# Layer two's memory attention between the first pair's projections, twelve gates last, and eight heads' sample state updated in the output stage

## The chip, the cores and the metric

The kernel runs on one core of one Trainium2 chip. The metric is the device time of one execution in microseconds (us), the median of several runs. A profile is taken of one further execution; its span is the time from that execution's first to its last instruction. Engines are named as in the profile: PE is TensorE, DVE is VectorE, ACT is ScalarE, POOL is GpSimd, SP is SyncE, which issues the loads.

## The reference, cut to what matters

One step of a two-layer trunk over 256 prompt tokens and 8 sample tokens (264 together), width 2048. Layer one mixes tokens by windowed attention; layer two, which the change is about, by a gated recurrence with 12 heads. Each layer has four memory heads beside that, a gate of the full width and an output projection:

```python
q, f, iv, mq, g = split(h @ w_in)                  # 12 + 12 + 12 + 4 + 16 column blocks of 128
fg = lb + (1 - lb) * sigmoid(f);  k = 1 - fg;  q = silu(q)
o, s_new = chunked recurrence over q, k, iv, log(fg), from s0      # prompt: s0 = 0; sample: s0 = state_hgrn
o = o * rsqrt(mean(o * o) + eps) * norm_w
mem_o = softmax(mq @ mk.T / sqrt(128)) @ mv        # prompt: mk, mv projected; sample: from the caches
y = (concat(o, mem_o) * silu(g)) @ w_out
h = layer_norm(ALPHA * h + y)
```

For a sample token the recurrence has one step: `s_new[b] = fg * s0[b] + k * v` for each of 8 sequences and 12 heads (a 128x128 matrix each). These 96 matrices are an output of the step. The token's own result needs `s0`, but not `s_new`.

## The kernel before, in words

**Units.** Almost all work is cut into units of one load each: 1 MB of weights or of a memory cache, or 512 KB of sample state. `Stream` (the class of lines 58 to 131) holds them in a list. A unit's load goes through the SP queue into one of four "raw" buffers in on-chip memory. `prep` then splits the float32 values into a high and a low half-precision part: ACT scales and rounds (line 97), DVE subtracts (line 98). The parts go to one of four "hl" buffers, or, for the last eight output units, to one of eight "held" buffers. PE multiplies with three passes (lines 303 to 305): high by high, high by low, low by high. A weight unit is 16 chunks of three matmuls with 264 columns. A raw buffer is free for another load when its split is done. A state unit's raw buffer is kept longer, as its new state is made in place and stored from there by POOL.

**Order.** The list gives the order in which units are written. A scheduler then places each instruction on its engine by its own simulated time, so neighbouring units mix, and it also picks which of the four raw buffers a load gets. On the chip every engine works through its list in order. The SP queue does too: a load that must wait for its buffer holds up all loads behind it. `pump` starts the next piece of side work (recurrence of a head pair, memory softmax of a head) after each unit.

**Layer two before.** Six pairs of heads come one after the other: f, f, v, v, then per head q, state and (heads 0 to 7) an early gate. `state_unit` computes the sample token's result from the state and then updates the state: 8 matmuls that spread v over partitions (`vb`, line 1233), 8 ACT scalings (line 1237), 8 DVE multiply-adds (line 1238), and the store. After the pairs come the four memory-query units, then eight cache units (`c_mk`, `c_mv`) which alternate with the eight late gates, and the memory softmax. A cache unit is split like a weight unit, but its 32 matmuls have one or two columns. The last stage is 16 output units: the projection (matmuls `o`), a residual addition (line 747) and two running sums (lines 764 and 765) on DVE. Output units 8 to 15 run first over 176 columns and, from the held buffers, again over the remaining 88 while the first part is normalised.

## Time and profile before

| | |
|---|---|
| median of 3 runs | 905.26 us (904.99 to 907.28) |
| the profiled execution's own time | 906.08 us |
| its span, first to last instruction | 904.3 us |
| busy: PE / DVE / ACT / POOL | 886.6 / 701.5 / 582.4 / 34.9 us |
| moved by DMA | 198.67 MB, 220 GB/s on average |

Layer two's first unit starts on PE at 420 us. The matmuls of the cache units (`mss`, `mso`) and of the late gates around them lie between about 729 and 803 us, and those of the output units (`o`) between 800 and 893 us. Matmuls are pipelined, so that a busy PE only says that some matmul was under way. The number of matmuls that started in a stretch says how fast PE really went. Below, rows give busy us in a window with the number of instructions behind it, or, for groups of instructions, the number, the busy time and the mean duration.

### The profile page before, as it was taken

What the parts mean: (1) busy time and instruction counts of PE and PEld (TensorE: products, weight loads), DVE (VectorE), ACT (ScalarE), POOL (GpSimd) and SP (SyncE); (2) the same over time, 40 slices, a digit from 0 to 9 for tenths busy, and PEclk for the clock granted to TensorE, in tenths of its full rate; (3) what the DMA queues carried; (4) which work ended last, traced back from release to release, by engine and by line L of the source; (5) the groups of instructions that cost most, each with busy time, mean ns of one, the idle gap of its engine ahead of it and who ended that gap; (6) DMA issues with size and microseconds to landing.
All of it is one profiled execution on the core that took longest, in us unless ns stands there. A gap on an engine that the chain in (4) does not pass through costs nothing.

```text
span 904.3 us, 21814 instructions
## 1 busy us (share of the span) xinstructions
PE 886.6 (98%) x9281; PEld 762.9 (84%) x9281; DVE 701.5 (78%) x1230; ACT 582.4 (64%) x982; POOL 34.9 (4%) x68
## 2 busy tenths in 40 slices
PE   9999999999999999999999999999999999799996
PEld 6888889678888888876888888898888888688996
DVE  6879877669886666697687887979788989678736
ACT  6767776657664444476766877777777585858415
POOL 1100010000000000002000000000000000000000
PEclk9999999999999999999999999999999999899999
DMA  9998566557785555556374655827454878456303
GB/s 340 392 353 317 188 245 209 188 208 265 262 333 192 187 192 203 207 198 214 127 292 137 216 201 174 299 101 260 160 215 164 303 283 308 172 207 244 130 2 97
DMA packets 37853, 198.67 MB, mean 220 GB/s; under 512 B 4555, under 2 KB 10732, under 8 KB 17532
## 3 DMA queue, kind: packets, MB, share of 16 engines
q1 hardware_dynamic: 33024, 181.55, 56.3%
q0 software_dynamic: 4688, 15.67, 4.6%
q8 instruction: 72, 1.18, 0.5%
q14 instruction: 25, 0.20, 0.1%
q10 hardware_dynamic: 44, 0.07, 0.0%
HBM read 180.03 MB, written 17.22 MB: 218 GB/s over the span
## 4 chain that ended last, share of the span: by engine, by line
PE 77%; DVE 8%; ACT 6%; DMA 6%; issue 3%; SPq 0%; ACTq 0%; DVEq 0%
PE o L303 5%; PE o L305 5%; PE o L304 5%; PE g L305 5%; PE g L303 5%; PE g L304 5%; DVE hl L98 4%; ACT hl L97 2%; PE hv L305 2%; PE hv L303 2%; PE hv L304 2%; DMA raw<-in_w_in 2%; PE hq L303 2%; PE hq L305 2%; PE hq L304 2%
## 5 line engine op out<-in xcount | busy, mean ns | idle before, releaser
L98 DVE SCALAR_TENSOR_TENSOR hl<-raw,hl 128x2048 f16<-128x2048 f32 (+2 forms) x168 | 358.6, 2138 | 82.0 <-ACT hl L97 81.0
L97 ACT ACTIVATE hl<-raw 128x2048 f16<-128x2048 f32 (+2 forms) x168 | 299.2, 1784 | 97.8 <-PE o L305 45.4
L305 PEld LDWEIGHTS <-hl 128*128 128x128 f16 (+2 forms) x2048 | 197.4, 98 | 31.8 <-DVE hl L98 2.9
L303 PEld LDWEIGHTS <-hl 128*128 128x128 f16 (+2 forms) x2048 | 197.3, 98 | 30.6 <-issue 2.2
L304 PEld LDWEIGHTS <-hl 128*128 128x128 f16 (+2 forms) x2048 | 197.4, 98 | 30.3 <-issue 2.2
L305 PE MATMUL g<-xhl,hl 128*128 128x264 f16 x512 | 142.0, 277 | 2.4 <-DVE hl L98 2.4
L303 PE MATMUL g<-xhl,hl 128*128 128x264 f16 x512 | 141.9, 277 | 0.0
L304 PE MATMUL g<-xhl,hl 128*128 128x264 f16 x512 | 141.9, 277 | 0.0
L303 PE MATMUL o<-mix,hl 128*128 128x264 f16 x384 | 105.4, 276 | 0.8 <-DVE xres L747 0.8
L304 PE MATMUL o<-mix,hl 128*128 128x264 f16 x384 | 105.8, 276 | 0.0
L305 PE MATMUL o<-mix,hl 128*128 128x264 f16 x384 | 105.7, 276 | 0.0
L303 PE MATMUL q<-xhl,hl 128*128 128x264 f16 x192 | 53.0, 276 | 1.0 <-DVE kst L251 1.0
L303 PE MATMUL f<-xhl,hl 128*128 128x264 f16 x192 | 52.9, 276 | 0.4 <-DVE mvhl L251 0.4
L305 PE MATMUL hv<-xhl,hl 128*128 128x264 f16 x192 | 53.0, 276 | 0.0
L303 PE MATMUL hq<-xhl,hl 128*128 128x264 f16 x192 | 53.0, 276 | 0.0
L304 PE MATMUL hq<-xhl,hl 128*128 128x264 f16 x192 | 53.0, 276 | 0.0
L305 PE MATMUL hq<-xhl,hl 128*128 128x264 f16 x192 | 53.0, 276 | 0.0
L304 PE MATMUL hv<-xhl,hl 128*128 128x264 f16 x192 | 53.0, 276 | 0.0
L303 PE MATMUL hv<-xhl,hl 128*128 128x264 f16 x192 | 53.0, 276 | 0.0
L304 PE MATMUL q<-xhl,hl 128*128 128x264 f16 x192 | 53.0, 276 | 0.0
L305 PE MATMUL q<-xhl,hl 128*128 128x264 f16 x192 | 53.0, 276 | 0.0
L304 PE MATMUL f<-xhl,hl 128*128 128x264 f16 x192 | 52.9, 276 | 0.0
(338 smaller groups left out, 1858.4 us busy)
## 6 DMA issues: line engine op xcount, KB each, us to landing
raw<-in_w_in SPq DMA_DIRECT2D x88, 1024.0 KB, 6.4
raw<-in_w_o SPq DMA_DIRECT2D x32, 1024.0 KB, 5.0
raw<-in_w_mk SPq DMA_DIRECT2D x8, 1024.0 KB, 4.9
raw<-in_w_mv SPq DMA_DIRECT2D x8, 1024.0 KB, 4.9
raw<-in_c_mk SPq DMA_DIRECT2D x8, 1024.0 KB, 5.1
raw<-in_c_mv SPq DMA_DIRECT2D x8, 1024.0 KB, 7.0
raw<-in_state SPq DMA_DIRECT2D x12, 512.0 KB, 5.4
out_ss<-raw POOLq DMA_DIRECT2D x12, 512.0 KB, 5.5
```

The lines of the kernel that those rows point to most:

```text
L97: hi = self.nc.scalar.activation(hl[:, 0, s], raw[:, s], AF.Copy, scale=scale)
L98: lo = self.nc.vector.scalar_tensor_tensor(hl[:, 1, s], raw[:, s], scale, hl[:, 0, s], op0=ALU.mult, op1=ALU.subtract)
L303: mm(out, lhs(0), rhs(0), start=start, stop=False)
L304: mm(out, lhs(0), rhs(1), start=False, stop=False)
L305: return mm(out, lhs(1), rhs(0), start=False, stop=stop)
```

## The change

It does four things, all in layer two.

1. The four memory-query units stand right behind head 0's f unit. The eight cache units stand among the other projections of heads 0 and 1: ck0, f1, ck1, ck2, v0, ck3, v1, q0, cv0, cv1, gate 0, cv2, cv3, q1, then the two state units. The prompt's memory softmax moves with them.
2. Early gates are left for heads 0, 2, 3 and 6. The other twelve gates come after the last pair, with 10 and 11 at the end.
3. Heads 4 to 11 don't update their sample state in `state_unit`. They store what the update needs (v rows, forget gate, key; 80 floats per partition) to device memory. Eight update units stand in the output stage, one after each of output units 0, 2, ... 14. Each loads the head's state a second time (512 KB) and the stored 40 KB into a raw buffer, and does the same 8 matmuls, 8 scalings, 8 multiply-adds and store as before. State units of these heads no longer hold their raw buffer.
4. When more than one piece of side work is waiting, two steps are pumped after a unit.

```diff
-NG1 = 8
+EARLY = (0, 2, 3, 6)
+LATER = tuple(range(4, HD))
+KEPT = P // 2 + 2 * TS
...
     def load(self, i):
...
+            if s is None:
+                for home, src in self.units[i][0]:
+                    self.nc.sync.dma_start(home(t), src)
+                continue
...
+    def update(h, R, vr, fgs, ks8, sel):
+        for g in range(2):
+            pvb = bank("pt", 2, f"vb{h}{g}")
+            for bb in range(4):
+                mm(pvb[:, bb * P : (bb + 1) * P], sel[:, 4 * g + bb], vr, start=True, stop=True)
+            for bb in range(4):
+                b = 4 * g + bb
+                s = R[:, b]
+                nc.scalar.activation(s, s, AF.Copy, scale=fgs[:, b : b + 1])
+                nc.vector.scalar_tensor_tensor(
+                    s, pvb[:, bb * P : (bb + 1) * P], ks8[:, b : b + 1], s, op0=ALU.mult, op1=ALU.add
+                )
+        nc.gpsimd.dma_start(ss_o[h // 2, :, h % 2 * TS * P : (h % 2 + 1) * TS * P], R.rearrange("p b v -> p (b v)"))
...
+    def update_unit(h):
+        def fn(raw):
+            if not late_sel:
+                late_sel.append(cp.tile([P, TS, P], F16, tag="ms", name="late_sel", bufs=2))
+                nc.sync.dma_start(late_sel[0], sel_d)
+            R = raw[:, : TS * P].rearrange("p (b v) -> p b v", b=TS)
+            k = raw[:, TS * P : TS * P + KEPT]
+            update(h, R, k[:, : P // 2].bitcast(F16), k[:, P // 2 : P // 2 + TS], k[:, P // 2 + TS :], late_sel[0])
...
+            if h in LATER:
+                tail = cur["vr"][:, i, P // 2 :]
+                nc.vector.tensor_copy(tail[:, :TS], fgs)
+                nc.vector.tensor_copy(tail[:, TS:], ks8)
+                nc.gpsimd.dma_start(kept[pi][:, i], cur["vr"][:, i])
+                return
+            update(h, R, vr, fgs, ks8, H["sel"])
...
+    w1("f", 0, f_unit(0))
+    for h in range(NM):
+        w1("mq", h, mem1_sides(mq_unit(h)) if h == NM - 1 else mq_unit(h))
+    cache(c_mk, ck_unit, 0)
+    w1("f", 1, f_unit(1))
+    cache(c_mk, ck_unit, 1)
+    cache(c_mk, ck_unit, 2)
+    w1("v", 0, hv_unit(0))
+    cache(c_mk, ck_unit, 3)
+    w1("v", 1, hv_unit(1))
+    w1("q", 0, hq_unit(0))
+    cache(c_mv, cv_unit, 0)
+    cache(c_mv, cv_unit, 1)
+    gate_of(0)
+    cache(c_mv, cv_unit, 2)
+    cache(c_mv, cv_unit, 3)
+    w1("q", 1, hq_unit(1))
+    state_of(0)
+    state_of(1)
...
     for i in range(NC):
         stream.add(wb(w_o[1], i), out_unit(1, i), home=hold if i >= NC - NSPLIT else None)
+        if i % 2 == 0 and i // 2 < len(LATER):
+            h = LATER[i // 2]
...
+            stream.add(srcs, update_unit(h), split=False)
...
-        pump(1)
+        pump(2 if len(side) > 1 and i > state_at[1] else 1)
```

How the order of instructions moves is shown at three places. In the rows, the number behind a load (`raw170`) is the unit's place in the whole list. In matmul outputs, `o18` is output unit 8 of layer two and `g110` its gate 10; lines of the new program are 8 to 13 higher than those of the old.

The first place is the SP queue in the output stage, with what each load waits for. Before, only weights stand there:

```order
L79 DMA raw166_11485<-in_w_o 128x2048
L79 DMA raw167_11544<-in_w_o 128x2048
L79 DMA raw168_11607<-in_w_o 128x2048
L79 DMA raw169_11666<-in_w_o 128x2048
L79 DMA raw170_11725<-in_w_o 128x2048
L79 DMA raw171_11784<-in_w_o 128x2048
```

Now, from output unit 9 (`raw170`) to output unit 13 (`raw176`):

```order
L88 DMA raw170_11650<-in_w_o 128x2048 [waits DMASW5_49,PE_49]
L88 DMA raw171_11652<-in_w_o 128x2048 [waits DMAHW2_49,DVE_49]
L86 DMA raw172_11654<-in_state 128x1024 [waits DMAHW7_49,DMAHW5_49,DVE_49]
L86 DMA raw172_11654<-kept4_95 128x80 [waits DMAHW0_49,DMASW6_49]
L88 DMA raw173_11798<-in_w_o 128x2048 [waits DMASW6_49,PE_49]
L88 DMA raw174_11800<-in_w_o 128x2048 [waits DMAHW6_49,DVE_49]
L86 DMA raw175_11802<-in_state 128x1024 [waits DMAHW3_49,DMAHW1_49,DVE_49]
L86 DMA raw175_11802<-kept5_96 128x80 [waits DMAHW4_49,DMASW7_49]
L88 DMA raw176_11946<-in_w_o 128x2048 [waits DMASW7_49,PE_49]
```

Between the output weights stand the state and the stored rows of heads 9 and 10. The loads of output units 9, 11 and 13 wait on a DMASW semaphore, which is a store by POOL: their raw buffers are those of the updates of heads 6, 7 and 8.

The second place is ACT around the last gates. The rows run from the Ln of the last pair's normalisation to gate 11; `hl158` and `hl159` are the splits of output units 1 and 2, and `raw160` is the update of head 5:

```order
L1193 ACT_TABLE_LOAD
L1193 ACTIVATE osq50_10801<-rms50_10865,eps_rms_83 128x264
L743 ACT_TABLE_LOAD
L743 ACTIVATE sil115_10990<-g115_10941 128x264
L106 ACTIVATE hl158_11051<-raw158_10808 128x2048
L1193 ACT_TABLE_LOAD
L1193 ACTIVATE osq51_10803<-rms51_10868,eps_rms_83 128x264
L1196 ACT_TABLE_LOAD
L1196 ACTIVATE osq50_10801<-osq50_10801 128x264
L1215 ACTIVATE raw160_10938<-raw160_10938 128x128 x8
L739 ACTIVATE mix_99<-sil115_10990 128x264
L1196 ACTIVATE osq51_10803<-osq51_10803 128x264
```

The normalisation of heads 10 and 11, which stood in the middle of the cache units before, now runs while PE does the last two gates, and two of these rows belong to other work: gate 15's tanh and the scalings of head 5's update.

The third place is DVE at the end of the value-cache units, in the first pair. `hl97` is the split of the last of them, `hl98` that of head 1's q, `hl99` to `hl101` those of the two states and of head 2's f:

```order
L1059 COPY vr0_6264<-hvr0_6362 128x128
L107 SCALAR_TENSOR_TENSOR hl97_6540<-raw97_6288,hl97_6540 128x2048
L744 SCALAR_TENSOR_TENSOR mix_99<-mix_99,g10_6582 128x264
L261 SCALAR_TENSOR_TENSOR mphl13_6427<-mpt13_6422,mphl13_6427 128x512
L1059 COPY vr0_6264<-hvr1_6499 128x128
L107 SCALAR_TENSOR_TENSOR hl98_6577<-raw98_6368,hl98_6577 128x2048
L710 TENSOR_REDUCE msos1_6703<-mso1_6507 128x32
L107 SCALAR_TENSOR_TENSOR hl99_6633<-raw99_6441,hl99_6633 128x1024
L107 SCALAR_TENSOR_TENSOR hl100_6668<-raw100_6505,hl100_6668 128x1024
L107 SCALAR_TENSOR_TENSOR hl101_6706<-raw101_6543,hl101_6706 128x2048
```

Head 1's q is split only behind the copy of its transposed v (`hvr1`), which PE makes near the end of the value-cache matmuls. Before, the last value-cache unit was followed by gates alone, and the states of heads 0 and 1 stood apart.

More of the change, by code (lines that the diff above doesn't have):

```diff
@@ L72, in parts @@
         n = 4 if i == 0 else 2 if i < 4 else 1
-        w = self.units[i][0].shape[1] // n
+        src = self.units[i][0]
+        if isinstance(src, list):
+            return [None]
+        w = src.shape[1] // n
         return [slice(k * w, (k + 1) * w) for k in range(n)]
@@ L1241, in fn, with w1 @@
-            nc.gpsimd.dma_start(ss_o[pi, :, i * TS * P : (i + 1) * TS * P], raw)
+            if h in LATER:
[5 more added lines that the diff above has]
+            update(h, R, vr, fgs, ks8, H["sel"])
         return fn
     state_at = {}
-    for pi in range(HD // 2):
+    def w1(part, i, fn):
+        stream.add(wb(w_in1, NB1[part] + i), fn)
@@ new lines, in state_of, with gate_of, cache, mem1_sides @@
+    def state_of(h):
+        state_at[h] = len(stream.units)
+        stream.add(state[h // 2][:, (h % 2) * TS * P : (h % 2 + 1) * TS * P], state_unit(h), SA, whole=h not in LATER)
+    def gate_of(h):
+        w1("g", h, early_gate(h) if h in EARLY else gate_unit(1, h))
+    def cache(c, unit, t):
+        stream.add(c[1, t], unit(1, t), SA)
+    def mem1_sides(fn):
+        return with_side(fn, [lambda h=h: memp_side(1, h) for h in range(NM)])
+    w1("f", 0, f_unit(0))
+    for h in range(NM):
+        w1("mq", h, mem1_sides(mq_unit(h)) if h == NM - 1 else mq_unit(h))
@@ L1247, in trunk_kernel @@
+    cache(c_mk, ck_unit, 0)
[14 more added lines that the diff above has]
+    state_of(1)
+    for pi in range(1, HD // 2):
         for part, unit in (("f", f_unit), ("v", hv_unit)):
@@ L1248, in trunk_kernel @@
             for i in range(2):
[L1249 removed]
+                w1(part, 2 * pi + i, unit(2 * pi + i))
         for h in (2 * pi, 2 * pi + 1):
[L1251 to L1255 removed]
```

56 lines of the change are left out of this document (19 added, 37 removed).

## The prediction, made before the changed kernel was run

> **What bounds the kernel now.** I read the first part of the page, then the busy times by stage, then PE's waits in the stage that stood out, then the chain of waits there.
>
> ```profile
> span 904.3 us, 21814 instructions
> PE 886.6 (98%) x9281; PEld 762.9 (84%) x9281; DVE 701.5 (78%) x1230; ACT 582.4 (64%) x982; POOL 34.9 (4%) x68
> ```
>
> PE is busy nearly always, so work taken from DVE or ACT is worth only what PE waits for it. The change leaves the matmuls as they are. The stages (columns: busy us of PE, weight loads, DVE, ACT, POOL, with counts; PE's granted clock; DMA share; GB/s) say where PE waits:
>
> ```profile
> 300.00:350.00 50.00, 50.00 (x447) 43.49 (x445) 33.62 (x39) 21.88 (x20) 0.00 (x0) 1.00 0.55 193
> 600.00:650.00 50.00, 50.00 (x534) 44.26 (x532) 42.93 (x85) 37.25 (x68) 1.61 (x3) 1.00 0.58 194
> 700.00:750.00 50.00, 49.96 (x592) 44.45 (x590) 44.63 (x77) 34.38 (x39) 1.61 (x3) 1.00 0.79 289
> 750.00:800.00 50.00, 44.50 (x517) 37.54 (x515) 42.70 (x65) 34.68 (x55) 0.54 (x1) 0.93 0.67 247
> 800.00:850.00 50.00, 49.23 (x451) 43.01 (x450) 40.31 (x45) 32.71 (x33) 0.00 (x0) 1.00 0.56 208
> 850.00:860.00 10.00, 10.00 (x135) 10.00 (x133) 4.78 (x14) 1.47 (x4) 0.00 (x0) 1.00 0.01 2
> ```
>
> The head pairs (600 to 650) leave PE no idle time, with two state updates and two gates per pair. The cache units with late gates (750 to 800) do: PE is idle for 5.5 us and its clock is 0.93, which costs another 0.07 x 50 = 3.5 us. The output stage loses 0.8 us. In it DVE is done early: from 850 us on almost nothing is loaded.
>
> PE's waits from 740 to 805 us, and the chain of waits there (start, us, what):
>
> ```profile
> PE g L305 <- DVE hl L98: 2.4, 2, 1.7
> PE hpo L1169 <- ACT st L1147: 1.5, 1, 1.5
> PE mback L677 <- DVE mrows L674: 1.0, 1, 1.0
> ```
>
> ```profile
> 754.59 4.40 DVE hl L98 x2
> 761.20 2.21 DVE hl L98
> ...
> 776.41 1.28 ACT L1183
> 777.71 0.85 ACT osq L1183 x2
> ```
>
> DVE is the bound, with splits of 2.2 us each. Behind them come the last pair's normalisation and the memory softmax, all late at once. The change spreads exactly this: the cache units go between projections, and the last pair's tail gets twelve gates of PE work for cover.
>
> **The change part by part.** *The cache stage* goes: -5.5 - 3.5 = **-9.0 us**. Twelve gates remain. Per gate PE needs 48 x 50/447 = 5.4 us, DVE one split and three operations of 0.43 like the second row below, 3.5 us, so nothing else waits. The output stage's 0.8 us is counted anew below: **-0.8**.
>
> ```profile
> L733 ACT ACTIVATE sil<-g 128x264 f32<-128x264 f32 x5 | 1.9, 383 | 4.4 <-PE g L305 4.4
> L734 DVE SCALAR_TENSOR_TENSOR sil<-sil,g 128x264 f32<-128x264 f32 x5 | 2.2, 431 | 0.0
> 602.90 0.23 DVE L1049 COPY vr<-hvr 128x128 f16<-128x128 f16 x1 [1.99 <-PE hvr L1048]
> L747 DVE SCALAR_TENSOR_TENSOR xres<-xres,o 128x176 f32<-128x176 f32 (+1 forms) x8 | 2.8, 348 | 14.6 <-PE o L305 14.6
> ```
>
> *The pairs* lose eight updates from DVE and ACT and gain two small copies and a 40 KB store by POOL per head; PE is covered there already (50.00 busy of 50), so 0. Without cover the copies would be some 0.2 us each, by the third row. Pumping two steps also costs 0 here: the pairs without a gate keep 5.4 us units to hide a step.
>
> *The first pair* takes in the eight cache units. A cache unit's 32 matmuls take little of PE. Windows with many of them:
>
> ```profile
> 774.00:778.00 4.00, 2.88 (x42) 2.32 (x41) 1.09 (x6) 3.47 (x8) 0.54 (x1) 1.00 0.83 285
> 778.00:780.00 2.00, 1.76 (x19) 1.31 (x19) 0.00 (x0) 1.97 (x4) 0.00 (x0) 0.53 0.05 21
> 782.00:784.00 2.00, 1.71 (x61) 1.42 (x57) 2.00 (x5) 2.00 (x3) 0.00 (x0) 1.00 0.00 0
> 784.00:786.00 2.00, 0.56 (x3) 0.43 (x4) 2.00 (x5) 2.00 (x3) 0.00 (x0) 0.74 0.00 0
> 786.00:788.00 2.00, 2.00 (x11) 1.36 (x10) 2.00 (x1) 2.00 (x6) 0.00 (x0) 0.50 0.64 201
> ```
>
> 61 in 1.71 us is 28 ns each, 0.9 us per unit against 2.2 us of DVE. Taken over the stretch from ck0 to head 1's q, six projections have 6 x (5.4 - 2.2) = 19 us of DVE to spare, and the cache units lack 8 x 1.3 = 10. But cv0 to cv3 come nearly in a row on PE (3.6 us). Then DVE has head 1's v copy (0.2) and q's split (2.2) left, and PE only 31 small matmuls, seven others of 0.11 and eight `vb` (about 2 us) before it needs that split: 0.5 us late. The two state splits and updates behind it make about 0.5 us more. The clock adds to this: twice it fell to about half (0.53, 0.50) behind windows full of small matmuls or gaps. A half-clock stretch like 778 to 781 costs some 1.7 us. The run of 3.6 us will hit one or not; I take 1.0. Together **+2.0** (0 to 4.5). The spare selector's load (256 KB, SP) stands ahead of the two states and waits until head 2's memory softmax is read. That is 13 us or more ahead of the states' turn, so 0; without that cover the states and f2 behind it come late by up to a state's load, 5.4 us (the row of page part 6 below).
>
> The Trainium skill, "TensorE: Matmul & The Clock Gate", section "HAM oscillation — how this bites in real kernels", puts the drop down to idle gaps above about 3.4 us. By that the run of small matmuls, which has no such gap, would cost nothing and the sum would be 1.0 us lower. The trace disagrees: PE was busy 1.71 us of 2.00 at 782, idle 1.4 us after it, and the clock was 0.50 at 786.
>
> *The turn to the output stage.* Now ACT ends the last pair's normalisation during the last two gates, 2 x 5.4 = 10.8 us. From its first table load to gate 10's tanh stand four table loads (1.28 each), two Ln, two Exp, three small operations of 0.4 (first row above), a split and the scalings of head 5's update:
>
> ```profile
> 536.17 2.34 ACT raw L1237 x8
> 515.43 1.38 DVE raw L1238 x5
> 459.94 0.45 PE vb L1233 x8
> ```
>
> 5.1 + 0.85 + 0.85 + 1.2 + 1.9 + 2.3 = 12.2 us, and DVE's product 0.4. Output unit 0 waits for the accumulator bank that this frees: 12.6 - 10.8, some **+1.6** (0 to 2.5).
>
> *The updates in the output stage.* PE's part is 0.45 us per head, as before elsewhere. What is new is a hand-over of a raw buffer. Output unit 9's load must wait for the store of head 6's update, 11 for head 7's, 13 for head 8's, 15 for head 9's. Rows for the steps:
>
> ```profile
> raw<-in_state SPq DMA_DIRECT2D x12, 512.0 KB, 5.4
> out_ss<-raw POOLq DMA_DIRECT2D x12, 512.0 KB, 5.5
> DMA to landing us min/median/max: 2.9/5.5/7.4
> L97 ACT ACTIVATE held<-raw x8: 1894/1910/1912, 823.6 to 845.4; 128x2048 f16<-128x2048 f32 x8
> L98 DVE SCALAR_TENSOR_TENSOR held<-raw,held x8: 2287/2290/2292, 825.5 to 848.2; 128x2048 f16<-128x2048 f32 x8
> DMA to landing us min/median/max: 4.8/5.4/6.8
> ```
>
> (The first landing row is the state store's, the second that of output weights from 803 us on.) From an update's `vb` to the split of the unit that gets its buffer: 8 multiply-adds at 1.38/5 are 2.2, store 5.5, load 5.4, ACT 1.9, DVE 2.3: H = 17.3 us. A held unit is 48 matmuls at 10/135 = 0.074, 3.6 us. PE's work in that time is
>
> - to unit 9: 3 x 5.4 + 3.6 + 2 x 0.45 = 20.7 us, not late;
> - to unit 11: 5.4 + 3 x 3.6 + 0.9 = 17.1, late 0.2;
> - to unit 13: 4 x 3.6 + 0.9 = 15.3, late 17.3 - 15.3 - 0.2 = 1.8;
> - to unit 15: 15.3 + 2.0, not late.
>
> That is 2.0 us; 0 with the shortest store and load (H = 14.1), 5.3 with the longest (H = 20.6). Behind a waiting load on SP stand the next unit's weights and the next state; behind the late split on DVE stand unit 12's residual and head 10's update, for which PE's next bank waits. DVE's own work from unit 8's end to unit 15's split is 5 x 2.2 + 4 x 2.2 + 6 x 3 x 0.3 (0.35 recorded, of which the next one overlaps some) = 25.2 us, PE's 6 x 3.6 + 4 x 0.45 = 23.4: 1.8 us over, of which about half falls into the same wait. Together **+2.9** (1.0 to 7.1). DMA bytes don't bind: 16 + 8 x 1.04 MB in some 78 us is 310 GB/s, and the page's slices reach 392:
>
> ```profile
> GB/s 340 392 353 317 188 245 209 188 208 265 262 333 192 187 192 203 207 198 214 127 292 137 216 201 174 299 101 260 160 215 164 303 283 308 172 207 244 130 2 97
> ```
>
> *Sum*: -9.0 - 0.8 + 2.0 + 1.6 + 2.9 = **-3.3 us**: span 901.0, own time 902.8 (the profiled run's 906.08 is 1.8 outside the span), and the same off the median of 905.26, whose runs lie within 2.3 us: **902.0 us**.
>
> **The rivals.** *A, the hand-over is hidden.* If stores land as fast as the fastest did (2.9), H is 14.1 and nothing waits for buffers; with the turn at 0, the first pair at 1.0 and DVE's 1.7 left the sum is -9.8 + 2.7 = -7.1: 898.2 us. For it: the stage moved 208 GB/s only. Against: store medians of 5.5 came at similar loads. The Trainium skill, "DMA: Bandwidth & Descriptors", "Anatomy of one DMA — SWDGE (gpsimd) path", fits 2.0 us plus bytes/436 KB, which would be 3.2 us for a store. That is an estimate from the page and near this case; the measured median speaks against it.
>
> *B, the stall moves into the first pair.* The four value caches need 4 x 2.2 = 8.8 us of DVE and give PE 3.6. If DVE has no lead there, PE waits the 5.2 us and then runs 1.7 us at half clock: 6.9 instead of 2.0, 906.9 us. For it: DVE was the bound for the same units (10 us of 10 in the stage that stalls is its usual reading). Against: four split buffers of lead, and gate and q units around.
>
> *C, slower: the SP queue.* Each late hand-over delays the loads behind it and, through unit 9, the next updates, so beyond H = 20.7 the wait grows twice as fast: 5.3 + 2 x (H - 20.7). At H = 24 (store 7.4, load 6.8, and two splits ahead on DVE) it is 11.9 instead of 2.0: -3.3 + 9.9 = +6.6, 911.9 us. It decides from H of about 22. For it: the longest store and load alone give 20.6. Against: it needs both of them in most hand-overs, where the medians are 10.9 together.
>
> **How the numbers follow.** About 0.3%, 2.7 us, is what a measurement of this kernel can tell from no change. Forecast 0.40 (own range 898.5 to 906; about two thirds of it faster, the rest the same), A 0.18, B 0.23 (nearly all the same), C 0.19. So faster 0.45, same 0.32, slower 0.23. The range 896 to 910 holds the forecast with all its bounds, A and B, and part of C.
>
> **What would show it.** Right: the windows that hold cache units and late gates have no idle PE and clock 1.00; PE's waits in the output stage are a few, behind splits of units 11 to 15 or residuals, 3 to 7 us in all; SP's longest waits there end with a POOL store. For the first pair, one or two waits near head 1's q, perhaps one half-clock stretch. Wrong: PE idle above 5 us in the first pair (B), stalls at every hand-over from unit 9 on (C), none at all after unit 8 (A), or idle PE in the pairs, which I cost at nothing.

## The result, and the profile after

The changed kernel takes 919.34 us (917.16 to 919.53) against 905.48 us for the kernel before on the same chip. The ratio is 1.0138, 95% interval 1.0123 to 1.0154: slower by 1.4%. The forecast was 902.0 us, with a range of 896 to 910. Its sign was wrong, and the time lies outside the range.

The first lines of the page of after, then its busy times by stage (columns: busy us of PE, weight loads, DVE, ACT, POOL, with counts; PE's granted clock; DMA share; GB/s):

```profile
span 917.6 us, 21905 instructions
PE 891.4 (97%) x9281; PEld 765.2 (83%) x9281; DVE 702.2 (77%) x1246; ACT 587.8 (64%) x986; POOL 39.3 (4%) x76
```

```profile
475.00:500.00 25.00, 23.56 (x315) 20.26 (x313) 16.85 (x32) 17.65 (x36) 0.00 (x0) 0.93 0.44 149
500.00:525.00 25.00, 21.93 (x235) 18.41 (x232) 20.40 (x36) 17.60 (x28) 1.08 (x2) 1.00 0.76 284
525.00:575.00 50.00, 48.08 (x512) 42.16 (x510) 43.57 (x89) 38.37 (x65) 1.61 (x3) 1.00 0.62 226
575.00:700.00 125.00, 125.00 (x1355) 111.10 (x1354) 100.91 (x197) 86.68 (x140) 4.88 (x9) 1.00 0.53 183
700.00:800.00 100.00, 99.39 (x1026) 87.25 (x1025) 79.19 (x130) 70.27 (x111) 2.16 (x4) 1.00 0.50 179
800.00:825.00 25.00, 24.49 (x225) 21.12 (x224) 17.52 (x31) 13.23 (x20) 1.08 (x2) 1.00 0.57 193
825.00:850.00 25.00, 23.81 (x238) 21.15 (x237) 16.99 (x34) 13.79 (x24) 1.07 (x2) 1.00 0.71 254
850.00:875.00 25.00, 18.79 (x219) 18.40 (x219) 18.78 (x41) 13.94 (x26) 1.07 (x2) 0.90 0.71 257
```

Two of the same stretches before the change:

```profile
500.00:525.00 25.00, 25.00 (x266) 22.10 (x264) 22.22 (x54) 20.00 (x31) 1.61 (x3) 1.00 0.64 213
700.00:800.00 100.00, 94.46 (x1106) 81.99 (x1104) 87.34 (x141) 69.05 (x94) 2.15 (x4) 0.97 0.73 268
```

From such rows I work out one number for each stage, its *loss*: the time in which PE is idle, plus the width times what the clock lacks to 1.00. For 850 to 875 that is 6.21 + 0.10 x 25 = 8.7 us. The number is rough, as stages shift by up to 13 us from kernel to kernel, but it tells where to look:

| stage (us of the span) | before | after | predicted change | found |
|---|---|---|---|---|
| first pair, 475 to 575 | 0.1 | 8.2 | +2.0 | +8.1 |
| pairs, 575 to 700 | 0.1 | 0.0 | 0 | 0 |
| 700 to 800 (caches and late gates before, gates now) | 8.5 | 0.6 | -9.0 | -7.9 |
| 800 to the end: the span's +13.3 less the rows above | | | +3.7 | +13.1 |

So the stage that the change was read to repair is repaired. Two others lose more than it gave. DVE has no more work in all (701.5 us busy before, 702.2 now); whether it has too much within one of these stages is tested below.

PE's waits in the output stage, and ACT's longest there (engine, line, what it waited for: total us, times, longest):

```profile
PE o L313 <- DVE xres L757: 3.9, 2, 3.7
PE o L313 <- ACT held L106: 2.5, 2, 1.5
PE o L315 <- DVE held L107: 2.0, 1, 2.0
```

```profile
ACT raw L1215 <- DMA raw<-kept: 20.0, 5, 4.5
```

ACT stands still for 20 us until the state and the kept rows of an update have arrived. The SP queue in the same stage says why it comes so late; here are its issues of state loads and of the two weight loads behind the first of them, and then the splits on DVE before them:

```profile
836.40 0.33 SPq L86 DMA_DIRECT2D raw<-in_state  x1
...
838.04 1.24 SPq L88 DMA_DIRECT2D raw<-in_w_o  x2
849.76 0.33 SPq L86 DMA_DIRECT2D raw<-in_state  x1
...
861.19 0.33 SPq L86 DMA_DIRECT2D raw<-in_state  x1
...
873.77 0.33 SPq L86 DMA_DIRECT2D raw<-in_state  x1
```

```profile
834.08 2.29 DVE L107 SCALAR_TENSOR_TENSOR hl<-raw,hl 128x2048 f16<-128x2048 f32 x1 [1.32 <-ACT hl L106]
...
847.44 2.29 DVE L107 SCALAR_TENSOR_TENSOR held<-raw,held 128x2048 f16<-128x2048 f32 x1 [2.09 <-ACT held L106]
...
858.87 2.29 DVE L107 SCALAR_TENSOR_TENSOR held<-raw,held 128x2048 f16<-128x2048 f32 x1 [0.54 <-ACT held L106]
...
871.45 2.29 DVE L107 SCALAR_TENSOR_TENSOR held<-raw,held 128x2048 f16<-128x2048 f32 x1 [1.78 <-ACT held L106]
```

The splits end at 836.37, 849.73, 861.16 and 873.74, and each time a state load leaves SP 0.03 us later. In the written program the two share a raw buffer: the load of head 8's update goes into the buffer of output unit 7, head 9's into that of unit 9. SP works in order, so the two weight loads behind it wait as well. The chain of waits shows the rest of one turn:

```profile
838.04 7.44 DMA raw<-in_w_o
845.50 1.92 ACT held L106
```

State load held until a split, weights behind it (7.44 us), ACT's part (1.92), DVE's split (2.29), next state load: 13.4, 11.4 and 12.6 us from one state load to the next. PE needs 2 x 3.6 + 0.45 = 7.7 us for the two short units and the update of such a turn.

The first pair has the same pattern with the stores. SP's waits from 500 to 521 us; then the load of the two states, the two stores that POOL issues with their time to landing, and SP's issues behind them; then what ACT waits for:

```profile
SPq L88 <- DMA out_ss<-raw: 13.4, 2, 7.9
```

```profile
474.30 6.97 SPq L88 DMA_DIRECT2D raw<-in_state  x2
...
500.05 0.54 POOL L1219 DMA_DIRECT2D out_ss<-raw  x1 [75.69 <-DVE qk L1265]
506.23 0.54 POOL L1219 DMA_DIRECT2D out_ss<-raw  x1 [5.63 <-DVE raw L1216]
...
DMA to landing us min/median/max: 5.9/7.5/9.2
...
506.00 0.80 SPq L88 DMA_DIRECT2D raw<-in_w_in  x2
...
515.45 1.90 SPq L88 DMA_DIRECT2D raw<-in_w_in  x2
```

```profile
511.75 1.91 ACT L106 ACTIVATE hl<-raw 128x2048 f16<-128x2048 f32 x1 [4.63 <-DMA raw<-in_w_in]
```

The stores land 5.9 and 9.2 us after their issue, at about 505.9 and 515.4. Each time a weight load leaves SP within 0.1 us of that, and ACT waits 4.63 us for the first of them. Head 0's state was loaded at 474.30: its buffer was taken for 31.6 us, and head 1's beside it. Two of four raw buffers were left for the projections.

**Theory 1** is this: a raw buffer that holds a state which is updated is taken until the store has landed, and in both places the loads behind it come late. In the first pair those loads wait for the store itself. In the output stage the effect is indirect: with a buffer taken by an update, the next state load waits for a weight's buffer, and weights wait behind that state load. The **rivals** are the amount of work on DVE and ACT, the order in which DVE has it, and full DMA engines.

### The profile page after: what moved, and what is told of

The parts are those of the page before. It is cut to its first block, busy times and chain, and to the rows that moved or that the text cites. A ratio compares the mean times of both kernels' runs of the same rounds, so it can differ in the third digit from the quotient of the medians.

```text
span 917.6 us, 21905 instructions
## 1 busy us (share of the span) xinstructions
PE 891.4 (97%) x9281; PEld 765.2 (83%) x9281; DVE 702.2 (77%) x1246; ACT 587.8 (64%) x986; POOL 39.3 (4%) x76
## 4 chain that ended last, share of the span: by engine, by line
PE 48%; issue 37%; DMA 7%; DVE 4%; ACT 3%; POOL 1%; SPq 0%; DVEq 0%; POOLq 0%; ACTq 0%
PE o L313 4%; PE o L315 4%; PE o L314 4%; DMA raw<-in_w_o 4%; PE g L313 3%; PE g L314 3%; PE g L315 3%; PE q L313 2%; PE q L314 2%; PE q L315 2%; DVE hl L107 2%; PE mq L314 2%; PE mq L313 2%; PE mq L315 2%; PE mk L314 2%
```

## The experiments

Losses by stage, worked out as above, for all kernels whose profiles are used below. The kernels were timed on several chips, each beside the kernel before on the same chip; the ratios below are to that. The losses are those of the one profiled execution, which lies up to 4.4 us off the median. The span less all its losses, those before 475 us included, is 879 to 884 us in all sixteen kernels, so the losses account for nearly all of the differences between the spans.

| kernel | median us | 475 to 575 | 575 to 700 | 700 to 800 | 800 to 875 | 875 to the end |
|---|---|---|---|---|---|---|
| before | 905.5 to 906.4 | 0.1 | 0.1 | 8.5 | 0.8 | 9.2 |
| after | 919.3 | 8.2 | 0.0 | 0.6 | 10.4 | 12.9 |
| order alone | 920.4 | 8.5 | 2.4 | 3.4 | 10.4 | 9.2 |
| deferral alone | 916.9 | 0.0 | 0.0 | 4.9 | 8.0 | 18.3 |
| states apart | 925.2 | 8.5 | 0.0 | 0.8 | 7.9 | 16.7 |
| four updates in split buffers | 910.6 | 8.1 | 0.0 | 0.6 | 5.1 | 9.7 |
| no store of heads 0 and 1 | 918.8 | 3.8 | 2.1 | 0.6 | 13.0 | 13.1 |
| one step | 924.0 | 8.8 | 2.0 | 0.3 | 16.6 | 12.9 |
| updates in the gates | 927.7 | 7.0 | 0.0 | 20.1 | 2.7 | 9.6 |
| updates spread | 937.0 | 6.3 | 1.4 | 14.9 | 10.8 | 14.8 |
| own places for updates | 912.4 | 8.9 | 0.0 | 0.5 | 5.7 | 12.8 |
| own places, heads 0 and 1 | 921.4 | 7.1 | 0.8 | 0.3 | 19.5 | 11.7 |
| own places, value caches apart | 909.5 | 2.4 | 1.6 | 0.8 | 7.9 | 12.2 |
| after, splits behind residuals | 920.2 | 9.3 | 0.0 | 0.6 | 9.9 | 15.0 |
| value caches apart, splits behind residuals | 907.8 | 2.4 | 1.5 | 0.7 | 4.8 | 11.9 |
| the same, two steps in the late gates only | 903.8 | 2.4 | 0.0 | 0.3 | 4.0 | 11.8 |

**Order alone, and deferral alone.**

```diff
-LATER = tuple(range(4, HD))
+LATER = ()
```

> The change's order of units (caches in the first pair, twelve gates last, two steps pumped), but every head's sample state is updated in its own pair, as before, and none in the output stage. Theory 1 (buffers): a state that is updated keeps its raw buffer until its store has landed; the first pair has two such states in a row, the output stage one per two units, and in both places the weights behind them come late. Then the output stage's 13 us of new loss go and the first pair's 9 us stay: 919 - 13 = about 906 us (904 to 908). Theory 2 (the first pair's loss is the two-step pump and the two copies per kept head, not the order): the first pair's loss stays too, but the pairs 1 to 5 show stalls as soon as their eight updates are back: above 909 us. My predicted terms alone (first pair +2.0, turn +1.6, cache stage -9.0) would give 900 us.

Measured: 920.43 us, ratio 1.0156 (1.0135 to 1.0177), where theory 1 gave 906 and my own terms 900. The first pair's 8.5 us stay, as theory 1 said. Theory 2's "above 909" holds, and its stalls in the pairs are there too, 2.4 us and part of the 3.4 behind them. (Its reason for the first pair falls below, with one step throughout.) But most of what the output stage gives back is lost at the turn:

```profile
800.00:825.00 25.00, 19.07 (x177) 16.34 (x176) 11.95 (x20) 12.51 (x19) 0.54 (x1) 0.91 0.37 133
...
PE o L313 <- ACT mix L739: 4.8, 1, 4.8
```

With the eight updates back in their pairs, the last pair's scan steps stand so late in the written-out order that its normalisation begins when the gates are through. So here the deferral kept the turn to the output stage free, and the parts do not add up. (It isn't the updates in the pairs alone: a kernel below updates heads 4 to 7 in their pairs and loses nothing at the turn.)

```diff
-EARLY = (0, 2, 3, 6)
+EARLY = tuple(range(8))
...
-    w1("f", 0, f_unit(0))
-    for h in range(NM):
-        w1("mq", h, mem1_sides(mq_unit(h)) if h == NM - 1 else mq_unit(h))
...
+    for pi in range(HD // 2):
...
         for h in (2 * pi, 2 * pi + 1):
             w1("q", h, hq_unit(h))
             state_of(h)
             if h in EARLY:
                 gate_of(h)
+    for h in range(NM):
+        w1("mq", h, mem1_sides(mq_unit(h)) if h == NM - 1 else mq_unit(h))
...
-        pump(2 if len(side) > 1 and i > state_at[1] else 1)
+        pump(1)
```

> The order of units before the change (caches between late gates after the pairs, eight early gates, one step pumped), with the updates of heads 4 to 11 in the output stage. Theory 1 (buffers): the output stage loses its 13 us, the cache stage its 10 us as before, the first pair nothing: 905.5 + 13 = about 918 us (915 to 921). Theory 2 (the stall of the output stage comes from what the new order leaves late for it, the last pair's normalisation and the late gates, not from the updates): little is lost there, 905 to 909 us. My predicted term for the updates alone (+2.9) would give 908 us.

Measured: 916.87 us, ratio 1.0118 (1.0081 to 1.0154), as theory 1 expected; most of the new loss stands at 850 to 900 us, with 3.8 and 8.0 us. The updates alone cost some 11 us (7 to 14 by the interval; the four runs lie far apart, 912.90 to 921.12, and the profiled one is the slowest). So they cost much in the old order as well, and theory 2 and my +2.9 are out. One thing differs from after: from 825 to 885 us SP waited 11.0 us for three stores here, and 1.2 us for one in after.

**Less time in the buffers?** The two states of the first pair apart:

```diff
     w1("q", 0, hq_unit(0))
+    state_of(0)
     cache(c_mv, cv_unit, 0)
...
-    state_of(0)
     state_of(1)
```

> The change, with head 0's state moved up to behind head 0's q, so that the two states of the first pair no longer stand in a row; the same units and the same work. Theory 1 (two of four raw buffers are held by updates at once, 474 to 515 us): one buffer more is free there, and the loads of head 2's and 3's f and v come earlier: the first pair's loss falls from about 10 to 4 to 6 us, the time to 913 to 916 us. Rival (the eight cache units' splits and the updates are more DVE work than the first pair covers): the work is unchanged, and so is the time, 918 to 921 us.

Measured: 925.19 us, ratio 1.0213 (1.0193 to 1.0233): worse, where theory 1 said better and the rival no change. The first pair lost as much as in after (8.5 against 8.2 us), but earlier: 6.3 us before 500 us, where after lost 3.2. Where the rest of the total went is not shown; the profiled execution was the fastest of the four (922.53 us). Issues of head 0's state load and of its store, of this kernel:

```profile
455.89 0.33 SPq L88 DMA_DIRECT2D raw<-in_state  x1
...
493.76 0.54 POOL L1219 DMA_DIRECT2D out_ss<-raw  x1 [67.61 <-DVE raw L1216]
```

A state that stands earlier in the list is loaded earlier, but its update is no earlier by as much: 37.9 us from load to store here, 25.8 in after (474.30 to 500.05). My expectation counted how many states are held at once, and not for how long.

```diff
-        nc.gpsimd.dma_start(ss_o[h // 2, :, h % 2 * TS * P : (h % 2 + 1) * TS * P], R.rearrange("p b v -> p (b v)"))
+        if h > 1:
+            nc.gpsimd.dma_start(ss_o[h // 2, :, h % 2 * TS * P : (h % 2 + 1) * TS * P], R.rearrange("p b v -> p (b v)"))
```

> The change without the stores of heads 0's and 1's updated state (that part of the output is left out; the updates themselves are still worked out). Theory 1 (a buffer is held until the store has landed): the first pair's two stores took 5.9 and 9.2 us, and two weight loads left SP 0.06 and 0.01 us after them. Without them the loads go when the updates end, 6 and 9.5 us earlier; PE's gaps between 503 and 523 us (4.2 us in all) shrink to 1 to 2, the half clock and the gap in front of it stay: 916 to 917 us. Rival (the first pair's loss is its DVE and ACT work in the order of the queues): nothing changes, 918.5 to 920.5 us.

This kernel leaves out those two stores, and with them a part of the output. Measured: 918.75 us, ratio 1.0138 (1.0119 to 1.0156). In the first pair theory 1 is right:

```profile
500.00:525.00 25.00, 24.03 (x250) 20.93 (x249) 22.55 (x41) 20.80 (x35) 0.00 (x0) 1.00 0.70 258
525.00:575.00 50.00, 50.00 (x549) 44.35 (x547) 44.08 (x89) 35.10 (x59) 1.62 (x3) 1.00 0.62 220
```

3.07 and 1.92 us of idle PE have become 0.97 and 0. PE's waits of `hs`, the scan's matmuls, for ACT are gone as well (3.8 us in 4 from 480 to 580 us in after, none here). The run also takes 1 MB off the DMA engines; that the buffers were what counted is seen from SP's waits for the two stores above. The total shows little of the 4.0 us: 2.1 come back as a loss in the pairs, and the output stage, which still has its updates, loses more. By the time alone this run would read as the rival.

**Is it the updates' buffers, or their work?** The next kernels do the same updates elsewhere. First, those of heads 8 to 11 (`own` is true for them) are loaded into split buffers, which are free by then:

```diff
+        if self.own(i):
+            t = self.pool.tile([P, 2, 2048], F16, tag="hl", name=f"up{i}", bufs=self.nsplit)
+            t = t.bitcast(F32).rearrange("p s w -> p (s w)")
+        else:
             t = self.pool.tile([P, 2048], F32, tag="raw", name=f"raw{i}", bufs=self.nraw)
```

> The change, with the last four update units (heads 8 to 11) loaded into the split buffers that nobody uses from output unit 8 on, so that the four raw buffers there hold weights only. Theory 1 (each group of three loads waits on SP for a split of the group before: cycles of 11.4 to 13.4 us for two units that need 7.7 us of PE): the loads run ahead, the half with short units loses 2 to 5 us instead of 13, and the time is 908 to 914 us. Rival A (DVE's own work: splits, residuals, sums and updates, 25.2 us against PE's 23.4 by my own count): unchanged work, 917 to 920 us. Rival B (the DMA engines are full, loads of 7.4 to 9.0 us): earlier issue makes each load longer, 917 to 920 us.

Measured: 910.61 us, ratio 1.0048 (1.0033 to 1.0063), as theory 1 expected. A stretch with short units and updates:

```profile
850.00:875.00 25.00, 25.00 (x339) 25.00 (x337) 24.88 (x51) 17.06 (x33) 2.12 (x4) 1.00 0.65 255
```

PE loses nothing, although DVE is busy for 24.88 us of 25. With weights in time, DVE carries all this work, if with nothing to spare. That settles both rivals of this run for the short units: neither DVE's work nor the DMA engines set the end there. The end of the kernel is back near its old loss too (9.7 us from 875 us on, against 12.9 in after and 9.2 before). Of the 5.1 us left, 4.6 lie at 825 to 850 us, with one wait of 2.9 us for a residual.

Then the same eight updates behind late gates, where DVE has time to spare:

```diff
-    for j in [j for j in range(NC) if j not in EARLY and j not in last] + list(last):
+    for n, j in enumerate([j for j in range(NC) if j not in EARLY and j not in last] + list(last)):
         gate_of(j)
+        update_of(n, (0, 1, 2, 4, 5, 6, 8, 9))
```

> The change with the same eight updates, two for every three of the first ten late gates, instead of in the output stage. Theory 1: the output stage's 13 us of new loss go, since its loads wait for no update any more. In the gates an update holds one of four raw buffers for about a load of 4, 4 us of work and a store of 4, and the other three carry a gate each for 16 us; DVE's work is 12 x 3.5 + 8 x 2.2 = 60 us of PE's 65. Cost there 0 to 5 us: 906 to 911 us, I take 907. Rival (an update costs its own DVE and ACT time wherever it stands beside splits): DVE's 60 of 65 us with the last pair's tail leaves 6 to 10 us of stalls in the gates, 912 to 917 us.

Measured: 927.68 us, ratio 1.0244 (1.0228 to 1.026), 17 us above the upper end of what theory 1 gave. The output stage is clean (2.7 us), the gates lose 20.1:

```profile
700.00:800.00 100.00, 84.94 (x869) 71.04 (x867) 74.86 (x161) 65.28 (x132) 5.35 (x10) 0.95 0.51 178
```

SP's waits from 740 to 795 us, its issues between 768 and 781, and one of the stores:

```profile
SPq L88 <- DMA out_ss<-raw: 34.1, 4, 11.5
...
768.17 0.33 SPq L86 DMA_DIRECT2D raw<-in_state  x1
...
780.65 0.33 SPq L88 DMA_DIRECT2D raw<-in_w_in  x1
...
777.60 0.53 POOL L1219 DMA_DIRECT2D out_ss<-raw  x1 [30.35 <-DVE raw L1216]
```

The mechanism is theory 1's at its clearest: from 768 to 780 us no weight is loaded, since the buffers hold states, and the loads wait 34.1 us for four stores. What failed is my 12 us per hold. An update runs when its turn comes on PE, ACT and DVE, so POOL stored nothing for 30.35 us, and the states that came early blocked buffers meanwhile (issued at 741.52 and 750.42 us, stored, if in the same order, at 777.60 and 780.91). The rival's reason, too much DVE work, is not what this shows: DVE is busy 75 us of 100, and from 740 to 802 us ACT waited 15.7 us for weights before it could split them.

```diff
-LATER = tuple(range(4, HD))
+LATER = (0, 1) + tuple(range(4, HD))
...
+        update_of(n, (1, 2, 4, 5, 7, 8))
...
+        update_of(i, (0, 2, 4, 6))
```

> The change with the updates of heads 0 and 1 deferred too: six updates behind late gates (1, 2, 4, 5, 7, 8 of twelve), four behind output units 0, 2, 4 and 6, none among the short units. Theory 1: both places lose their held buffers: the first pair's 10 us fall to 3 to 5 (half clock and the value caches stay), the output stage's 15 to 2 to 4, the gates lose 0 to 3: 919.3 - 6 - 12 + 1.5 = about 903 us (900 to 906). Rival (the first pair's loss comes from the cache units' own splits and their order): it keeps 8 to 10 us, 907 to 911 us.

With heads 0 and 1 deferred as well (six updates behind gates, four behind output units): 937.01 us, ratio 1.035 (1.0328 to 1.0372). The stage from 500 to 525 us loses nothing any more, but ten updates in raw buffers cost 15 us in the gates and 11 behind them. The expectation was wrong for the same reason.

**Places of their own.** The split activations are not read after the last gate. Their memory holds three updates, and POOL can load them, so that SP and the raw buffers see weights only:

```diff
+        if self.own(i):
+            at = NC * T - ((self.nown + 2) % 3 + 1) * (TS * P + KEPT)
+            t = self.room[:, at : at + TS * P + KEPT]
...
-                    self.nc.sync.dma_start(home(t), src)
+                    self.nc.gpsimd.dma_start(home(t), src)
...
+        update_of(i, (1, 2, 4, 5, 7, 9, 11, 13))
```

> The change with its eight update units in three places of their own (the room of the split activations, which nobody reads after the last gate) instead of the raw buffers, loaded and stored by POOL, behind output units 1, 2, 4, 5, 7, 9, 11 and 13; SP and the four raw buffers serve weights only. The work is the same. Theory 1 (buffers held by updates, and the SP queue behind them): the output stage's loss falls from 15 to 1 to 3 us: 919.3 - 13 = 906 us (904 to 909). Rival A (an update costs its DVE and ACT time in the output stage): in the short units DVE has 8 x 3.2 + 3 x 2.2 = 32 us of work against PE's 30, in the long ones 37 against 45; if that decided, a few microseconds stay, but the loss already seen there would stay too: 912 to 917 us. Rival B (POOL's own queue, where a load waits for the store of the update three before): updates come late, PE waits for their accumulator banks, 909 to 914 us.

Measured: 912.35 us, ratio 1.0069 (1.0052 to 1.0086): 7 us better than after, where 13 were expected, and a time that both rivals named as well. The trace sorts them. PE waits for updates 0.5 us in all, which is not rival B. From 800 to 875 us the loss falls from 10.4 to 5.7, from 875 to 900 us from 2.0 to 0, so the short units carry the updates, which is not rival A. This run changes three things at once, the buffers, the queue and the units behind which the updates stand; the kernel with split buffers, which changed little but the buffers, is the cleaner proof. Of the 5.7 us left, 3.4 are one wait for a residual, between long and short units. It is taken up below.

```diff
-LATER = tuple(range(4, HD))
+LATER = (0, 1) + tuple(range(6, HD))
```

> As room8, but the heads updated in the output stage are 0, 1 and 6 to 11: the first pair keeps no buffer for an update, and heads 4 and 5 are updated in their own pair. Theory 1: the first pair's loss between 500 and 575 us goes from 7 to 1 to 2 (the value caches' 3.6 before 500 stay); the third pair takes two updates, as before the change: room8's time less 5, about 901 us (899 to 904). Rival (the first pair's loss is cache splits and order): no gain there, room8's time or up to 2 us above, 905 to 908 us.

Measured: 921.37 us, ratio 1.0173 (1.014 to 1.0205); a miss. The stretch from 500 to 525 us loses 0.0 instead of 2.8 us, as theory 1 said. But with heads 4 and 5 updated in their pair the turn loses 13.4 us, much as in the run with the order alone.

```diff
-    cache(c_mv, cv_unit, 0)
-    cache(c_mv, cv_unit, 1)
...
-    cache(c_mv, cv_unit, 2)
-    cache(c_mv, cv_unit, 3)
...
         for i in range(2):
             w1(part, 2 * pi + i, unit(2 * pi + i))
+            if pi == 1:
+                cache(c_mv, cv_unit, 2 * p + i)
...
+LATER = (0, 1, 2, 3) + tuple(range(8, HD))
```

> As room_first, with the four value-cache units one by one between the second pair's f and v, and the updates of heads 0 to 3 and 8 to 11 in the output stage (so neither pair with caches updates a state). Theory 4 (the 3.6 us that the first pair loses before 500 us come from four value caches in a row: their splits leave PE waiting, then the clock is halved for 3.4 us): they go, as each has a projection beside it: 898 us (895 to 902). Rival (the same splits crowd the second pair, where DVE then has about 47 of 54 us of work): a stall of 3 to 6 us there, 901 to 907 us.

(Head 0's state also stands before gate 0 again, and heads 4 to 7 are updated in their pairs.) Measured: 909.53 us, ratio 1.0038 (1.0025 to 1.0052). In the first pair both causes are gone now:

```profile
475.00:500.00 25.00, 25.00 (x262) 22.00 (x260) 17.50 (x35) 12.94 (x22) 1.08 (x2) 1.00 0.61 223
500.00:525.00 25.00, 25.00 (x352) 22.29 (x350) 24.49 (x27) 20.33 (x27) 0.00 (x0) 1.00 0.77 265
825.00:850.00 25.00, 20.40 (x179) 18.09 (x177) 22.57 (x39) 17.80 (x29) 3.20 (x6) 0.88 0.92 333
```

The eight cache units fit between projections without loss where no two value caches stand in a row and no buffer is held. From 550 to 575 us 2.4 us are lost, on waits of `hs`, where after lost 1.9 us; the rival's stall behind splits did not come. At the turn (800 to 825 us) nothing is lost, although four heads are updated in their pairs. The time is 7.5 us above the expected 895 to 902, and the output stage, the third row, is where they are: 4.6 + 0.12 x 25 = 7.6.

**The residual behind splits.** In that row PE waits 4.6 us for one residual. DVE around it:

```profile
PE o L330 <- DVE xres L775: 4.6, 1, 4.6
...
839.90 2.28 DVE L119 SCALAR_TENSOR_TENSOR held<-raw,held 128x2048 f16<-128x2048 f32 x1
...
842.78 2.29 DVE L119 SCALAR_TENSOR_TENSOR held<-raw,held 128x2048 f16<-128x2048 f32 x1
844.98 0.43 DVE L775 SCALAR_TENSOR_TENSOR xres<-xres,o 128x264 f32<-128x264 f32 x1
```

The order on DVE, written out ahead of time, has splits of later units before the residual. Here DVE goes from one split to the next without idle time, and the residual comes when they are done. (If their weights were late, DVE would wait for those first.) One rule takes that away, tried on after and on the last kernel:

```diff
+    def behind(self, i):
+        return self.issue_after(self.last) if self.last and self.units[i][6] else nullcontext()
...
-            lo = self.nc.vector.scalar_tensor_tensor(
+            with self.behind(i):
+                lo = self.nc.vector.scalar_tensor_tensor(
```

(`last` is the latest residual of layer two, and `units[i][6]` is set from output unit 8 on.)

> The change, where DVE's split of an output unit from the ninth on is issued only behind the latest residual (that of about four units before), so that no residual stands behind splits whose loads are late; the work and the buffers are the same. Theory 5 (the order on DVE makes the stall at 849 us): its 3.9 us and the half clock behind it, 1.7 us, go: 919.3 - 5.6 = about 914 us (912 to 916). Rival (the loads, late behind held buffers, are the bound of the whole cycle of 11 to 13 us): the stall only moves to the next split, 917 to 921 us.

Measured: 920.19 us, ratio 1.0153 (1.0134 to 1.0171): no gain, as the rival expected.

```profile
PE o L319 <- DVE xres L763: 5.1, 2, 4.0
```

While buffers are held, changing the order on DVE gains nothing; the wait for residuals is no shorter (5.1 us, 3.9 in after).

> room_cv with the same rule for DVE's splits. Theory 5: with buffers of their own for the updates nothing else is late there, so the wait of 4.6 us and the half clock behind it, 1.7 us, go: 909.5 - 6.3 = about 903 us (901.5 to 905). Rival (DVE has too much work there in any order): the wait comes back at a later unit, 908 to 911 us.

Measured: 907.77 us, ratio 1.001 (0.9999 to 1.0022); at 825 to 850 us the loss is 3.5 instead of 7.6. So the order counts once the loads are in time. The time is 2.8 us above the expected 901.5 to 905, since a wait of 2.8 us for a residual is left.

**Side steps.**

```diff
-        pump(2 if len(side) > 1 and i > state_at[1] else 1)
+        pump(1)
```

> The change with one side step per unit throughout, as before the change. Theory 3 (two steps in a row leave PE nothing between them, hence the waits of hs for ACT's qk, 3.5 us in 4, and for osq, 0.8): they go, and the steps come later, which the pairs have room for: 914 to 917 us. Rival A (those waits stand behind late loads on ACT's queue, theory 1): no change, 918 to 921 us. Rival B (the backlog of the memory softmax's steps in the first pair runs into the twelve gates and the turn): above 922 us.

One step throughout, on after: 923.99 us, ratio 1.0209 (1.0184 to 1.0234), rival B. The waits of `hs` did not go (2.9 us in 3 against 3.5 in 4), and the first pair lost 8.8 us, no less than in after: there they go with the held buffers, as the run without two stores showed. From 800 to 825 us the loss was 12 us. The second step that the change pumps is needed, at least late.

```diff
-        pump(2 if len(side) > 1 and i > state_at[1] else 1)
+        pump(2 if len(side) > 1 and i > state_at[HD - 1] else 1)
```

> room_cv_ord with two side steps per unit only in the late gates, one in the pairs. Theory 3 (the pairs' waits of hs for ACT's qk, 4.7 us in 6 in room_cv, come from two steps without a projection between them): the loss of the windows at 550, 650 and 700, 6.5 us, falls to about 1.5: 898 us (896 to 901). Rival (steps that come later push the last pair's tail into the turn, as with one step throughout): 903 to 910 us.

Measured on top of the kernel with 907.77 us: **903.76 us** (901.66 to 906.08), ratio 0.9974 (0.9961 to 0.9986) to before. Theory 3 expected 896 to 901, a gain of 5; it was 4.0. The pairs' 1.5 us of loss are gone, and nothing was lost at the turn. The 2.4 us before 575 us, which theory 3 counted in, stayed; the stages of the two profiles differ by 2.8 us in all.

This kernel beats both, if by no more than the 0.3% that the prediction named as the bound. Of the 8.5 us that the cache stage lost before, it keeps about a third.

## Why the prediction was wrong

- **Cache stage, -9.0: right.** Loss 8.5 before, 0.6 after.
- **Pairs, 0: right.** What I had not seen: updates in the pairs cost nothing before, but in two kernels with the new order (order alone, and heads 4 and 5) the last pair's steps came late at the turn. With the value caches apart and heads 4 to 7 updated in their pairs they did not, so this needs more than the updates.
- **First pair, +2.0 (0 to 4.5): found +8.1.** I went through DVE's work and the clock, and about the states I asked only whether their loads come in time ("13 us or more ahead of the states' turn, so 0"). I did not ask what they keep from others. Held buffers cost about 4 us of it, by the run without two stores. The value caches' part, 3.2 us, was forecast in kind: PE waited for splits there, and the clock halved (1.7 us, the price I had worked out, of which the sum took 1.0). Rival B had that mechanism, but not the larger one.
- **Turn, +1.6: 0.2 found** (0.5 against 0.3 from 800 to 825 us). The direction can't be told from so little. (12.6 - 10.8 is 1.8, not 1.6.)
- **Updates in the output stage, +2.9 (1.0 to 7.1): found about 13, with the end of the kernel.** This is the step that failed. It followed one hand-over, from a store to the weights that get its buffer, H = 17.3 us. In after that hand-over was hardly late: SP waited 1.2 us for a store from 825 to 885 us, by the first row below. (With the deferral alone it was late, by the 11.0 us above, so which hand-over binds depends on what precedes.) The one that bound goes the other way, from a weight unit's split to the state load that gets *its* buffer, with the next two weight loads behind it on SP. It turns in 11.4 to 13.4 us per two units, for 7.7 us of PE. Two sizes were off as well. Weight loads took 5.4 us in the rows that I used; from 836 to 880 us in after they take 7.7 (second row), and the stores 3.6 where I had 5.5 (third row). In H the two nearly cancel (17.7 us), so they are not why the term failed. The three rows:

```profile
SPq L88 <- DMA out_ss<-raw: 1.2, 1, 1.2
```

```profile
DMA to landing us min/median/max: 6.0/7.7/9.0
...
DMA to landing us min/median/max: 3.0/3.6/7.0
```

  Some 3.7 us of the 13 lie behind 875 us, for which the prediction had no term. "DMA bytes don't bind" was true and beside the point.
- **Rival A (hidden)** had the right store and the wrong conclusion. **Rival C** was the nearest, in its mechanism too: an SP queue in which a late load delays all behind it. I let it decide only from H of 22 us on, because I sought the delay in stores.
- **The signs.** PE was idle for 6.4 us in the first pair, B's sign, and the output stage stalled from hand-over to hand-over, C's sign; both came, each mainly from a cause that the rival didn't name.
- **A slip in rival A.** With the fastest store alone H is 14.7; 14.1 needs the fastest load too. Either is under 15.3, so the conclusion was the same.

The Trainium skill, "DMA: Bandwidth & Descriptors", "Anatomy of one DMA — SWDGE (gpsimd) path", gave 3.2 us for a store, an estimate by its fit. The output stage of after agrees better (median 3.6) than the row of before that I preferred to it (5.5).

Open is why the written-out order puts the last pair's steps so late in two kernels with more work in the pairs and not in a third; no run changed that alone. Not tested is whether the output stage could also be repaired by another place of the state loads in SP's queue, with the updates left in the raw buffers. Open too is the remaining 3.6 us at 825 to 850 us of the best kernel: PE waits there for residuals (2.1 us) and for update operations that free an accumulator bank (1.7 us), and what makes these late was not tried.

## What to carry to other kernels

When work that updates data in place is moved, count for how long it keeps its buffer, from the load's issue to the store's landing, and how many buffers the loads beside it are left with; idle engines at the new place don't help if the buffer is taken. On an in-order load queue ask of each load what its buffer waits for, since everything behind it waits too. And read an experiment by the stage it aims at: here a repaired stage gave its gain back elsewhere three times, and the total alone would have told the opposite.

## What the runs showed of the hardware

Two rows of after, side by side around the four value caches (the clock is the first number behind the counts):

```profile
480.00:487.80 7.80, 7.15 (x150) 6.61 (x149) 4.12 (x8) 4.63 (x6) 0.00 (x0) 1.00 0.21 69
487.80:491.20 3.40, 3.40 (x42) 2.62 (x39) 3.40 (x5) 2.62 (x5) 0.00 (x0) 0.50 0.82 277
```

The clock was half for 3.4 us, although PE had been idle for only 0.65 us of the 7.8 before, with many short matmuls in them (150 in 7.15 us); with the value caches one by one (502 to 519 us; the row of 500 to 525 us of that kernel, above) it stayed at 1.00. The rule on idle gaps above about 3.4 us in the Trainium skill, "TensorE: Matmul & The Clock Gate", section "HAM oscillation — how this bites in real kernels", would not have put a drop there. Elsewhere in after the clock was half from 853.0 to 856.4 us, behind a stretch (849 to 853 us) in which PE was busy for 0.33 us of 4.

Loads that start together are slow together: 1 MB took 6.0 to 9.0 us in the output stage of after, where it shares the time with a state, the kept rows and a store, at 254 to 257 GB/s over the stretch. The Trainium skill, "SBUF — State Buffer", "Can I just issue two DMAs to hit both halves?", says that two transfers at once share the same 16 engines; these loads agree with that. But 333 GB/s went through at the same place with the value caches apart (the row of 825 to 850 us above), so the rate of after was not the most that could be moved.
